# A transformer step on one core: the cross and feed-forward norms split into a gain ahead of the products and a root behind them, and their sums taken from GpSimd to VectorE

## The chip, the cores and the metric

The kernel runs on one core of a Trainium2 chip. Its engines are TensorE (matrix products, "PE" in the profile, its weight loads "PEld"), VectorE ("DVE"), ScalarE ("ACT"), GpSimd ("POOL") and SyncE ("SP", which issues the transfers). Each engine works through its own instructions in order and waits for the others by semaphores. The metric is the device time of one execution in microseconds. Three runs of the kernel before took 2624.62 to 2628.29 us, with a median of 2626.17.

## The reference, cut to what matters

One decoder layer for 2048 prompt tokens and 64 sample tokens, 1024 channels, all in float32:

```python
def _rmsnorm(x, g):
    return x * rsqrt(mean(x * x, axis=-1, keepdims=True) + 1e-5) * g

h = _rmsnorm(x, g_mix);  q, k, v, u = split(h @ w_in)          # windowed attention and pooling mixer
x = x + concatenate([attn_o, pool_o]) @ w_out
h = _rmsnorm(x, g_cross)
s = einsum('blhd,bmhd->bhlm', h @ w_cq, mem_k) * 256 ** -0.5   # 4 heads, 256 memory tokens
x = x + einsum('bhlm,bmhd->blhd', softmax(s), mem_v) @ w_co
h = _rmsnorm(x, g_ffn)
x = x + square(relu(h @ w_up)) @ w_down                        # hidden width 4096
y = _rmsnorm(x, g_final)
```

The root of a norm is one number per token. It is a factor of a whole row of `h`, so it can be applied to a product of `h` as well as to `h`: `(r * x * g) @ w = r * ((x * g) @ w)`. ReLU lets a positive factor through.

## The kernel before, in words

The tokens are cut into three superblocks of two blocks each: 384 + 384, 384 + 384, and 256 + (256 prompt and 64 sample) tokens. Activations lie with channels on the partitions and tokens along the columns. Every float32 product is made of three products of rounded parts: each operand is split into `hi` (a rounded copy) and `lo` (what is left), and hi x hi, hi x lo and lo x hi are added up in PSUM.

Weights come as 128x1024 pieces: a transfer into one of six `f` buffers, a cast on ScalarE (line 136, the `hi` part), and a subtraction on VectorE (line 137, the `lo` part), into two of twelve `w` buffers. `Stream` emits these ahead of the products that need them. When a dense stage has processed its last chunk, `S.behind` holds the residual add and the square of that chunk, and the casts emitted next are kept behind these two instructions (`issue_after`).

A superblock goes through these stages:

- norm 1 of both blocks, the "in" projection, windowed attention, pooling;
- `wo`, a dense stage of eight output chunks. A chunk of one block is 24 products (eight channel groups times three). `evac` of a chunk adds the product to `x` on VectorE (line 903) and calls `Norm.sq`;
- cross attention: per 128 tokens and pair of heads 24 products against the pieces "A" (the query weights and memory keys multiplied together beforehand), then a softmax: maximum (949) and its scale (950) on VectorE, exponentials on ScalarE (952), reciprocal (953), the scale of the probabilities on GpSimd (955), transposes on TensorE (931). The sample tokens have a path of their own;
- "B", a dense stage like `wo` (adds at line 1105);
- the feed-forward stage: eight groups of `up` (four chunks for both blocks) and `down`. The evacuation of an up chunk is ReLU on ScalarE (1143), its square on GpSimd (1144), a cast on ScalarE (1146) and a subtraction on VectorE (1147). The residual adds of `down` are line 1177. Norm 1 of the next superblock is worked in around `down(6)` and `down(7)`; the final norm (1194) follows `down(7)`.

A norm is built in three steps. `sq` squares a chunk on ScalarE (210) and adds it to an accumulator on GpSimd (211). `fin` sums the accumulator over the partitions with a product against a matrix of ones (220), then takes the root: logarithm and exponential on ScalarE (223, 224) and a correction step on VectorE (225 to 227). `apply` makes the operand of the next products: x times gain times root on VectorE (238), the `hi` cast on ScalarE (239), and the `lo` subtraction (241), which alternates between VectorE and GpSimd.

The order on each engine comes from a scheduler that places the instructions by the order of the program and by dependences; a few are pinned (`keep_in_program_order`, `issue_after`). `dense` goes through chunks and blocks as `order(nch, head, tail)` says: the first `head` chunks for block 0 and then for block 1, the middle ones in pairs, the last `tail` chunks again first for block 0 and then for block 1. What comes `after` a block (its `fin` and `apply`) is started one chunk after the block's last. There are four PSUM banks for dense products (`mm`), four for the rest (`aux`), eight `t` buffers of 400 columns for what VectorE, ScalarE and GpSimd pass on, and sixteen `act` buffers for operands.

Of the kernel before, what the change touches and what calls it, by code (L numbers as in the profile page):

```python
# [14 lines left out]
P = 128  # L15
# [36 lines left out]
def kernel(ctx: ExitStack, tc: tile.TileContext, io, nW=12, nF=6, nT=8):  # L52
# [30 lines left out]
    kcar = sb("kcar", 512, F32R)  # L83
    vt = sb("vt", 1024, F32R)
# [30 lines left out]
    class Stream:  # L115
        def __init__(self):
            self.items = deque()
            self.ready = deque()
            self.resW = 0
            self.resF = 0  # L120
            self.behind = []
# [4 lines left out]
        def emit(self):  # L126
# [6 lines left out]
            with ExitStack() as held:  # L133
                for i in self.behind:
                    held.enter_context(tc.issue_after(i))
                nc.scalar.copy(th[:], r[:, 0:1024])  # L136
                eng.tensor_tensor(tl[:], r[:, 0:1024], f32(th[:]), ALU.subtract)  # L137
# [50 lines left out]
    class Norm:  # L188
        def __init__(self, n, x, on_pe=False, add=None):
            self.n, self.x, self.on_pe, self.add = n, x, on_pe, add or nc.gpsimd  # L190
            self.acc = None
            self.pm = AUX.get() if on_pe else None

        def sq(self, k, eng=None):
            n = self.n
            i = None
# [11 lines left out]
            else:  # L208
                t = TS.get()
                i = nc.scalar.activation(t[:, 0:n], self.x(k), AF.Square)  # L210
                self.add.tensor_tensor(self.acc[:, 0:n], self.acc[:, 0:n], t[:, 0:n], ALU.add)  # L211
                TS.put(t)
            return i
# [17 lines left out]

        def apply(self, g, hi, lo, piece=8):
            n = self.n
            for k in range(8):
# [5 lines left out]
                eng = nc.vector if k % 2 == 0 else nc.gpsimd  # L240
                eng.tensor_tensor(lo(k), t[:, 0:n], f32(hi(k)), ALU.subtract)  # L241
                TS.put(t)
            TS.put(self.r)

# [28 lines left out]
    def dense(keys, blks, hi, lo, evac, head=2, tail=3, after=None, piece=8, seq=None):  # L273
# [3 lines left out]
        for c, b in seq or order(nch, head, tail):  # L277
# [13 lines left out]
            last = evac(c, b, ps)  # L291
            S.behind = last or []
# [75 lines left out]
    def prologue():  # L368
# [32 lines left out]
        for name, dst in (("ck", io["mk"]), ("cv", io["mv"])):  # L401
            a = Act(256)
            outs.append(a)
            for c in range(8):
                th, tl = S.next((name, c))
                ps = MM.get()
                if name == "ck" and c == 0:
                    with tc.issue_after(wu.ins):
                        mm3(ps[:, 0:256], range(8), lambda k: w8(th)[:, k, :], lambda k: w8(tl)[:, k, :], hm.hi, hm.lo)
                else:  # L410
# [80 lines left out]
    def superblock(s, blks, nxt):  # L491
# [409 lines left out]
        def add_evac(c, b, ps):  # L901
            bl = blks[b]
            i = nc.vector.tensor_tensor(bl.x(c), ps[:, 0:bl.n], bl.x(c), ALU.add)
            j = bl.norm.sq(c)
            return [i.ins, j.ins] if (c, b) == (7, 1) else None
# [13 lines left out]
        run(dense([("wo", s, c) for c in range(8)], blks, mix_hi(0), mix_hi(1), add_evac, head=3, after=after_out))  # L919
# [4 lines left out]
        def cross():  # L924
# [53 lines left out]
        def sample_cross():  # L978
# [11 lines left out]
            for i in range(2):  # L990
                nc.scalar.copy(qs[0:64, 512 * i:512 * i + 512], qq[i][0:64, :])
# [32 lines left out]
            nc.vector.tensor_scalar(t[:, 2:4], t[:, 0:2], -1.0 / 16, None, ALU.mult)  # L1024
            for g in range(2):
                nc.scalar.activation(pp[:, 256 * g:256 * g + 256], spv[:, g, :], AF.Exp, bias=t[:, 2 + g:3 + g], scale=1.0 / 16, accum_out=t[:, 4 + g:5 + g])
# [76 lines left out]
        def add_evac2(c, b, ps):  # L1103
            bl = blks[b]
            i = nc.vector.tensor_tensor(bl.x(c, 0, bl.np), ps[:, 0:bl.np], bl.x(c, 0, bl.np), ALU.add)  # L1105
            j = bl.norm.sq(c)
            return [i.ins, j.ins] if (c, b) == (7, 1) else None

        def after_co(b):
# [4 lines left out]
            bl.h3 = Act(bl.n)  # L1114
            yield from bl.norm.apply(V_GFFN, bl.h3.hi, bl.h3.lo, PIECE[2][b])

        for bl in blks:
            bl.norm = Norm(bl.n, bl.x)
            bl.nfull = bl.n
# [231 lines left out]
```

## Time and profile before

| | |
|---|---|
| median of three runs (lowest, highest) | 2626.17 us (2624.62, 2628.29) |
| profiled execution, its span | 2623.82 us, 2622.0 us |
| mean granted TensorE clock | 0.994 |
| TensorE busy | 2562.3 us, 98% |
| VectorE, ScalarE, GpSimd busy | 1300.5, 982.8, 657.9 us |
| squares of ReLU on GpSimd (1144) | 192 instructions, 216.4 us |
| sums of the norms on GpSimd (211) | 161 instructions, 182.2 us |
| bytes moved, mean rate | 244.76 MB, 93 GB/s |

In the rows of the profile "L211" is line 211, `t<-t,t` is the output and the inputs by the program's names, then partitions x elements and the type, then the count. A wait row names the waiting engine and line, then the engine and line that ended the wait, then the total, the number of times and the longest, in us. A window row begins with its start and end and its length, and then gives the busy time of PE, PEld, DVE, ACT and POOL with counts, the granted clock, the share of the DMA engines, and GB/s. A timeline row begins with start and duration.

### The profile page before, as it was taken

What the parts mean: (1) busy time and instruction counts of PE and PEld (TensorE: products, weight loads), DVE (VectorE), ACT (ScalarE), POOL (GpSimd) and SP (SyncE); (2) the same over time, 40 slices, a digit from 0 to 9 for tenths busy, and PEclk for the clock granted to TensorE, in tenths of its full rate; (3) what the DMA queues carried; (4) which work ended last, traced back from release to release, by engine and by line L of the source; (5) the groups of instructions that cost most, each with busy time, mean ns of one, the idle gap of its engine ahead of it and who ended that gap; (6) DMA issues with size and microseconds to landing.
All of it is one profiled execution on the core that took longest, in us unless ns stands there. A gap on an engine that the chain in (4) does not pass through costs nothing. (4 is left out here: it accounts for less than half of the span.)

```text
span 2622.0 us, 39268 instructions
## 1 busy us (share of the span) xinstructions
PE 2562.3 (98%) x15753; PEld 2457.1 (94%) x15753; DVE 1300.5 (50%) x2283; ACT 982.8 (37%) x1923; POOL 657.9 (25%) x723
## 2 busy tenths in 40 slices
PE   9899999999999999999999999999999999999998
PEld 8799989999999999897999999999999669999998
DVE  8567453533333367936363333334765645344334
ACT  6666342422222244824342222223464444322231
POOL 2215322411111152433241111113334214111111
PEclk9999999999999999999999999999999999999999
DMA  7833111211221123131111211112414572222210
GB/s 280 263 122 117 62 49 51 86 61 63 65 65 65 57 73 106 57 120 57 65 64 65 65 60 62 65 57 70 145 58 149 184 278 100 81 82 88 82 57 37
DMA packets 92539, 244.76 MB, mean 93 GB/s; under 512 B 16772, under 2 KB 31556, under 8 KB 91204
## 3 DMA queue, kind: packets, MB, share of 16 engines
q1 hardware_dynamic: 92356, 242.25, 27.9%
q8 instruction: 123, 2.02, 0.3%
q14 instruction: 60, 0.49, 0.1%
HBM read 219.53 MB, written 22.69 MB: 92 GB/s over the span
## 5 line engine op out<-in xcount | busy, mean ns | idle before, releaser
L286 PE MATMUL mm<-act,w 128*128 128x384 f32 (+2 forms) x2784 | 901.1, 324 | 2.8 <-ACT act L642 1.6
L287 PE MATMUL mm<-act,w 128*128 128x384 f32 (+2 forms) x2784 | 897.0, 322 | 3.4 <-POOL act L241 1.5
L288 PE MATMUL mm<-act,w 128*128 128x384 f32 (+2 forms) x2784 | 895.6, 322 | 1.4 <-DVE w L137 1.4
L136 ACT CAST w<-f 128x1024 fp32r<-128x1024 f32 x330 | 344.3, 1049 | 702.7 <-PE mm L112 457.6
L137 DVE TENSOR_TENSOR w<-f,w 128x1024 fp32r<-128x1024 f32 x330 | 418.4, 1276 | 305.7 <-ACT w L136 304.8
L111 PE MATMUL mm<-act,w 128*128 128x384 f32 (+2 forms) x1728 | 552.3, 320 | 2.8 <-DVE t L394 2.2
L113 PE MATMUL mm<-act,w 128*128 128x384 f32 (+2 forms) x1728 | 548.8, 318 | 1.9 <-DVE w L137 1.9
L112 PE MATMUL mm<-act,w 128*128 128x384 f32 (+2 forms) x1728 | 548.5, 317 | 0.0
L287 PEld LDWEIGHTS mm<-act,w 128*128 128x128 f32 x2784 | 525.7, 189 | 12.7 <-POOL act L241 3.7
L286 PEld LDWEIGHTS mm<-act,w 128*128 128x128 f32 x2784 | 525.8, 189 | 7.6 <-issue 2.3
L288 PEld LDWEIGHTS mm<-act,w 128*128 128x128 f32 x2784 | 525.6, 189 | 2.2 <-DVE w L137 2.0
L1144 POOL TENSOR_TENSOR t<-t 128x384 f32<-128x384 f32 (+2 forms) x192 | 216.4, 1127 | 1038.6 <-ACT t L1143 1038.6
L1177 DVE TENSOR_TENSOR x<-mm,x 128x384 f32<-128x384 f32 (+2 forms) x384 | 199.7, 523 | 327.5 <-PE mm L113 327.5
L111 PEld LDWEIGHTS mm<-act,w 128*128 128x128 f32 x1728 | 326.8, 189 | 4.7 <-ACT t L207 2.4
L113 PEld LDWEIGHTS mm<-act,w 128*128 128x128 f32 x1728 | 326.8, 189 | 2.4 <-DVE w L137 2.3
L112 PEld LDWEIGHTS mm<-act,w 128*128 128x128 f32 x1728 | 326.9, 189 | 1.1 <-issue 0.3
L211 POOL TENSOR_TENSOR t<-t,t 128x384 f32<-128x384 f32 (+2 forms) x161 | 182.2, 1132 | 337.0 <-ACT t L210 329.6
L1147 DVE TENSOR_TENSOR act<-t,act 128x384 fp32r<-128x384 f32 (+2 forms) x192 | 101.4, 528 | 295.5 <-ACT act L1146 295.4
L1146 ACT CAST act<-t 128x384 fp32r<-128x384 f32 (+2 forms) x192 | 93.5, 487 | 233.6 <-POOL t L1144 233.6
L210 ACT ACTIVATE t<-x 128x384 f32<-128x384 f32 (+2 forms) x140 | 68.0, 498 | 161.7 <-DVE x L1105 74.5
L111 PE MATMUL mm<-w,act 128*128 128x512 f32 x288 | 116.5, 407 | 9.7 <-ACT w L136 9.7
L1143 ACT ACTIVATE t<-mm 128x384 f32<-128x384 f32 (+2 forms) x192 | 88.3, 460 | 92.5 <-PE mm L288 88.6
(187 smaller groups left out, 2216.9 us busy)
## 6 DMA issues: line engine op xcount, KB each, us to landing
f<-in_wup SPq DMA_DIRECT2D x96, 512.0 KB, 3.5
f<-in_wdn SPq DMA_DIRECT2D x96, 512.0 KB, 3.5
f<-in_win SPq DMA_DIRECT2D x30, 512.0 KB, 3.8
f<-a_s SPq DMA_DIRECT2D x24, 512.0 KB, 3.5
f<-b_s SPq DMA_DIRECT2D x24, 512.0 KB, 4.7
x<-in_x SPq DMA_DIRECT2D x6, 1536.0 KB, 6.9
f<-in_wco SPq DMA_DIRECT2D x16, 512.0 KB, 5.4
f<-in_cmk SPq DMA_DIRECT2D x16, 512.0 KB, 4.3
```

The source lines that it names most:

```text
L111: nc.tensor.matmul(ps, Wh(k), Hh(k), start=first and i == 0, stop=False)
L112: nc.tensor.matmul(ps, Wh(k), Hl(k), start=False, stop=False)
L113: nc.tensor.matmul(ps, Wl(k), Hh(k), start=False, stop=final and i == last)
L136: nc.scalar.copy(th[:], r[:, 0:1024])
L137: eng.tensor_tensor(tl[:], r[:, 0:1024], f32(th[:]), ALU.subtract)
L211: self.add.tensor_tensor(self.acc[:, 0:n], self.acc[:, 0:n], t[:, 0:n], ALU.add)
L286: nc.tensor.matmul(ps[:, 0:n], w8(th)[:, k, :], hi(b, k), start=k == 0, stop=False)
L287: nc.tensor.matmul(ps[:, 0:n], w8(th)[:, k, :], lo(b, k), start=False, stop=False)
L288: nc.tensor.matmul(ps[:, 0:n], w8(tl)[:, k, :], hi(b, k), start=False, stop=k == 7)
L1144: nc.gpsimd.tensor_tensor(q[:, 0:n], r[:, 0:n], r[:, 0:n], ALU.mult)
L1147: nc.vector.tensor_tensor(lo, q[:, 0:n], f32(hi), ALU.subtract)
L1177: nc.vector.tensor_tensor(bl.x(m), ps[:, 0:n], bl.x(m), ALU.add)
```

## The change: what it does

For the cross and the feed-forward norm `apply` is gone. The evacuation of each `wo` and `B` chunk now also makes the operand of the next stage from gain times `x`, without the root: `hi` on ScalarE and `lo` on VectorE (`gain`). The root comes in behind the products. For the cross stage `fin_cols` makes it as a column per 128 tokens (one-column products with the accumulator as weights) and it becomes the scale of the exponentials and of the maximum; the sample queries are scaled by it when they are copied. For the feed-forward stage the root stays a tile (`r3`, in one of the eight `t` buffers for each block through the whole stage), and VectorE takes maximum with zero and times root in one instruction; the square moves from GpSimd to ScalarE. All sums of all norms go from GpSimd to VectorE, and in norm 1 all `lo` subtractions are on VectorE. The weight casts are no longer held behind the last square. `wo` has tail 2 (before 3), `B` tail 2 (before 4), `up(0)` head 2 (before 4).

```diff
-            with ExitStack() as held:
-                for i in self.behind:
-                    held.enter_context(tc.issue_after(i))
-                nc.scalar.copy(th[:], r[:, 0:1024])
-                eng.tensor_tensor(tl[:], r[:, 0:1024], f32(th[:]), ALU.subtract)
+            nc.scalar.copy(th[:], r[:, 0:1024])
+            eng.tensor_tensor(tl[:], r[:, 0:1024], f32(th[:]), ALU.subtract)
...
-            self.n, self.x, self.on_pe, self.add = n, x, on_pe, add or nc.gpsimd
+            self.n, self.x, self.on_pe, self.add = n, x, on_pe, add or nc.vector
...
+        def fin_cols(self, c):
+            pm = AUX.get()
+            w = (self.n + P - 1) // P
+            for i in range(w):
+                m = min(P, self.n - P * i)
+                tc.keep_in_program_order(nc.tensor.matmul(pm[0:m, i:i + 1], self.acc[:, P * i:P * i + m], ones[:, 0:1], start=True, stop=True))
+            TS.put(self.acc)
...
+            v, y, t = c[:, 8:8 + w], c[:, 12:12 + w], c[:, 16:16 + w]
+            nc.scalar.activation(t, v, AF.Ln, bias=eps[:])
+            nc.scalar.activation(y, t, AF.Exp, scale=-0.5)
...
+            nc.vector.tensor_scalar(c[:, 0:w], y, 1.0 / 16, None, ALU.mult)
+            nc.vector.tensor_scalar(c[:, 4:4 + w], y, -1.0 / 16, None, ALU.mult)
...
-                eng = nc.vector if k % 2 == 0 else nc.gpsimd
-                eng.tensor_tensor(lo(k), t[:, 0:n], f32(hi(k)), ALU.subtract)
+                nc.vector.tensor_tensor(lo(k), t[:, 0:n], f32(hi(k)), ALU.subtract)
...
+    def gain(bl, act, k, g):
+        gk = vec[:, g + k:g + k + 1]
+        nc.scalar.activation(act.hi(k), bl.x(k), AF.Copy, scale=gk)
+        nc.vector.scalar_tensor_tensor(act.lo(k), bl.x(k), gk, f32(act.hi(k)), ALU.mult, ALU.subtract)
...
-            i = nc.vector.tensor_tensor(bl.x(c), ps[:, 0:bl.n], bl.x(c), ALU.add)
-            j = bl.norm.sq(c)
-            return [i.ins, j.ins] if (c, b) == (7, 1) else None
+            nc.vector.tensor_tensor(bl.x(c), ps[:, 0:bl.n], bl.x(c), ALU.add)
+            gain(bl, bl.h2, c, V_GCROSS)
+            bl.norm.sq(c)
...
-            bl.norm.fin()
             ACTS.put(*bl.q, *bl.d)
-            bl.h2 = Act(bl.n)
-            yield from bl.norm.apply(V_GCROSS, bl.h2.hi, bl.h2.lo, 8 if last and b else PIECE[1][b])
+            bl.rc = RC[b]
+            bl.norm.fin_cols(bl.rc)
...
-                        nc.vector.tensor_scalar(t[:, 2:4], t[:, 0:2], -1.0 / 16, None, ALU.mult)
+                        i = c0 // P
+                        nc.vector.tensor_scalar(t[:, 2:4], t[:, 0:2], bl.rc[:, 4 + i:5 + i], None, ALU.mult)
                         for h in range(2):
-                            nc.scalar.activation(Pt[:, 256 * h:256 * h + 256], psv[:, h, :], AF.Exp, bias=t[:, 2 + h:3 + h], scale=1.0 / 16, accum_out=t[:, 4 + h:5 + h])
+                            nc.scalar.activation(Pt[:, 256 * h:256 * h + 256], psv[:, h, :], AF.Exp, bias=t[:, 2 + h:3 + h], scale=bl.rc[:, i:i + 1], accum_out=t[:, 4 + h:5 + h])
...
-            bl.h3 = Act(bl.n)
-            yield from bl.norm.apply(V_GFFN, bl.h3.hi, bl.h3.lo, PIECE[2][b])
+            bl.r3 = bl.norm.r
...
-                nc.scalar.activation(r[:, 0:n], ps[:, 0:n], AF.Relu)
-                nc.gpsimd.tensor_tensor(q[:, 0:n], r[:, 0:n], r[:, 0:n], ALU.mult)
+                nc.vector.scalar_tensor_tensor(r[:, 0:n], ps[:, 0:n], 0.0, bl.r3[:, 0:n], ALU.max, ALU.mult)
+                nc.scalar.activation(q[:, 0:n], r[:, 0:n], AF.Square)
```

The order of the instructions moves with it. In these listings a number behind a name is that of the buffer, and the lines of the changed kernel are its own. ScalarE at the end of `wo` in superblock 0, before: the squares of chunks (L210), the `hi` casts of the norm (L239) and then the three weight casts for "A" (L136).

```order
L210 ACTIVATE t_100<-x_106 128x384
L239 CAST act_76<-t_102 128x384
L239 CAST act_76<-t_98 128x384
L239 CAST act_76<-t_104 128x384
L239 CAST act_76<-t_101 128x384
L210 ACTIVATE t_97<-x_106 128x384
L136 CAST w_79<-f_92 128x1024
L136 CAST w_87<-f_93 128x1024
L136 CAST w_88<-f_94 128x1024
```

The same place in the changed kernel, where L206 is the square, L133 the weight cast, L266 the gain, and L243 and L244 are the root as a column:

```order
L206 ACTIVATE t_101<-x_105 128x384
L266 ACTIVATE act_76<-x_105,vec 128x384
L206 ACTIVATE t_97<-x_105 128x384
L133 CAST w_87<-f_93 128x1024
L266 ACTIVATE act_64<-x_106,vec 128x384
L206 ACTIVATE t_99<-x_106 128x384
L243 ACTIVATE rc_132<-rc_132,eps 128x3
L244 ACTIVATE rc_132<-rc_132 128x3
L133 CAST w_88<-f_94 128x1024
L266 ACTIVATE act_64<-x_106,vec 128x384
L206 ACTIVATE t_102<-x_106 128x384
```

The cast into `w_87` now stands ahead of the last two gains and squares, the cast into `w_88` ahead of the last one, and the cast into `w_79` further ahead than is shown.

VectorE at the end of superblock 0, before: the final norm of block 0 (L1194, eight instructions), residual adds of block 1 (L1177) and weight splits (L137); the sums are on GpSimd.

```order
L227 SCALAR_TENSOR_TENSOR t_103<-t_98,t_103 128x384
L1194 SCALAR_TENSOR_TENSOR x_105<-x_105,vec,t_103 128x384 x8
L1177 TENSOR_TENSOR x_106<-mm_107,x_106 128x384
L1177 TENSOR_TENSOR x_106<-mm_108,x_106 128x384
L1177 TENSOR_TENSOR x_106<-mm_109,x_106 128x384
L137 TENSOR_TENSOR w_82<-f_96,w_83 128x1024
L137 TENSOR_TENSOR w_84<-f_91,w_85 128x1024
L97 TENSOR_TENSOR w_80<-mm_110,w_79 64x384
```

The same place in the changed kernel, where L1199 is the residual add, L1216 the final norm, L134 the split and L207 a sum:

```order
L222 SCALAR_TENSOR_TENSOR t_103<-t_100,t_103 128x384
L1199 TENSOR_TENSOR x_106<-mm_107,x_106 128x384
L1216 SCALAR_TENSOR_TENSOR x_105<-x_105,vec,t_103 128x384 x8
L207 TENSOR_TENSOR t_101<-t_101,t_102 128x384
L1199 TENSOR_TENSOR x_106<-mm_108,x_106 128x384
L1199 TENSOR_TENSOR x_106<-mm_109,x_106 128x384
L134 TENSOR_TENSOR w_82<-f_96,w_83 128x1024
L207 TENSOR_TENSOR t_101<-t_101,t_104 128x384
L134 TENSOR_TENSOR w_84<-f_91,w_85 128x1024
L207 TENSOR_TENSOR t_101<-t_101,t_99 128x384
```

Three sums of block 1 now stand between its last residual adds and the weight splits, and one add has gone ahead of the final norm of block 0.

More of the change, by code (lines that the diff above doesn't have):

```diff
@@ L83 @@
     kcar = sb("kcar", 512, F32R)
+    RC = [sb(f"rc{i}", 20) for i in range(2)]
     vt = sb("vt", 1024, F32R)
@@ L290, in dense @@
                     yield
-            last = evac(c, b, ps)
-            S.behind = last or []
+            evac(c, b, ps)
             MM.put(ps)
@@ L406, in prologue @@
                 ps = MM.get()
[L407 to L410, printed above, removed]
+                with ExitStack() as held:
+                    if (name, c) == ("ck", 0):
+                        held.enter_context(tc.issue_after(wu.ins))
                     mm3(ps[:, 0:256], range(8), lambda k: w8(th)[:, k, :], lambda k: w8(tl)[:, k, :], hm.hi, hm.lo)
@@ L911, in after_out @@
             bl = blks[b]
[L912 removed]
             ACTS.put(*bl.q, *bl.d)
[L914 to L915 removed]
+            bl.rc = RC[b]
+            bl.norm.fin_cols(bl.rc)
         for bl in blks:
             bl.norm = Norm(bl.n, bl.x)
[L919 removed]
+            bl.h2 = Act(bl.n)
+        run(dense([("wo", s, c) for c in range(8)], blks, mix_hi(0), mix_hi(1), add_evac, head=3, tail=2, after=after_out))
         for bl in blks:
@@ L1104, in add_evac2 @@
             bl = blks[b]
-            i = nc.vector.tensor_tensor(bl.x(c, 0, bl.np), ps[:, 0:bl.np], bl.x(c, 0, bl.np), ALU.add)
-            j = bl.norm.sq(c)
-            return [i.ins, j.ins] if (c, b) == (7, 1) else None
+            nc.vector.tensor_tensor(bl.x(c, 0, bl.np), ps[:, 0:bl.np], bl.x(c, 0, bl.np), ALU.add)
+            gain(bl, bl.h3, c, V_GFFN)
+            bl.norm.sq(c)
         def after_co(b):
```

28 lines of the change are left out of this document (18 added, 10 removed).

## The prediction

> **What bounds the kernel now.** I first read the page's busy line and the list of what the engines wait for.
>
> ```profile
> PE 2562.3 (98%) x15753; PEld 2457.1 (94%) x15753; DVE 1300.5 (50%) x2283; ACT 982.8 (37%) x1923; POOL 657.9 (25%) x723
> ```
>
> TensorE computes for 2562.3 of the 2622.0 us, and the change leaves it the same large products. So only the 59.7 us in which TensorE is idle, and any small products added, can move the time. Next I read TensorE's waits (total, times, longest), whole span:
>
> ```profile
> PE mm L111 <- ACT w L136: 9.9, 7, 3.0
> PE aux L220 <- POOL t L211: 7.9, 4, 2.7
> PE aux L931 <- POOL cp L955: 2.5, 4, 0.8
> ```
>
> The second row is the sum of a norm, still being added up on GpSimd when TensorE reaches the product that reads it. The first row is weight casts that come too late, and the third is softmax tiles. The same view by window says where. First the start of the cross stage (from 300 us in superblock 0, from 1190 in 1; both have this row):
>
> ```profile
> PE mm L111 <- ACT w L136: 2.4, 1, 2.4
> ```
>
> The start of the cross stage in superblock 2 (2036 to 2062 us):
>
> ```profile
> PE mm L112 <- DVE w L137: 2.3, 1, 2.3
> PE aux L112 <- DVE act L974: 1.3, 1, 1.3
> PE mm L111 <- ACT w L136: 0.7, 1, 0.7
> PE aux L113 <- POOL act L241: 0.6, 1, 0.6
> ```
>
> The start of the feed-forward stage in superblock 2 (2188 to 2212); the same place in superblocks 0 and 1 has the third row alone, with the same 0.5:
>
> ```profile
> PE aux L220 <- POOL t L211: 1.4, 1, 1.4
> PE mm L287 <- DVE act L241: 0.8, 2, 0.4
> PE mm L287 <- POOL act L241: 0.5, 1, 0.5
> PE mm L286 <- ACT act L239: 0.2, 1, 0.2
> ```
>
> The two block ends, where the next superblock's first norms and the final norm run under the last down products: at 985 to 1012 us
>
> ```profile
> PE aux L220 <- POOL t L211: 1.3, 1, 1.3
> PE mm L286 <- DVE x L1177: 0.5, 1, 0.5
> ```
>
> and at 1860 to 1885 the first of these two rows again with 2.5 (the second is the same, 0.5):
>
> ```profile
> PE aux L220 <- POOL t L211: 2.5, 1, 2.5
> ```
>
> Last the prologue, at 66 to 82 us the sum, and at 98 to 114 the weights:
>
> ```profile
> PE aux L220 <- POOL t L211: 2.7, 1, 2.7
> ```
>
> ```profile
> PE mm L111 <- ACT w L136: 3.5, 2, 3.0
> PE mm L112 <- DVE w L137: 0.8, 1, 0.8
> ```
>
> All of these except the last two rows are waits for work that the change removes, shortens or moves.
>
> **The change part by part.**
>
> *The cross norm no longer stands between wo and the cross products.* ScalarE's timeline shows why the weight cast is late:
>
> ```profile
> 319.13 0.52 ACT L210 ACTIVATE t<-x 128x384 f32<-128x384 f32 x1 [0.49 <-DVE x L903]
> 319.56 2.93 ACT L136 CAST w<-f 128x1024 fp32r<-128x1024 f32 x3
> ```
>
> The three casts are held behind the last square. Afterwards one is done before, the next stands ahead of the last two gains and squares, and none is held, so the 2.4 us go twice. The L931 waits (2.5 us in all, these two superblocks) come from softmax steps queued on VectorE among the eight L238 and eight L241 of the second block. Those are gone; I take all 2.5. Sum 7.3. In superblock 2 the same hold and the same norm cost 0.7 + 2.3 + 1.3 + 0.6 = 4.9. There I leave 0.5, because a late gain on ScalarE now stands ahead of the last sample cast: 4.4.
>
> *The feed-forward norm.* All rows of L220, L241 and L239 before the up products go: 1.4 + 0.8 + 0.5 + 0.2 + 2 x 0.5 = 3.9. The up products start on gain times x; the root is first needed by VectorE one chunk later.
>
> *The sums on VectorE.* Seven sums of 256 columns ran there before (minimum, median, maximum ns):
>
> ```profile
> L211 DVE TENSOR_TENSOR t<-t,t x7: 418/422/425, 6.7 to 16.6; 128x256 f32<-128x256 f32 x7
> ```
>
> and a two-input instruction of 384 columns, the residual add, takes (sum, mean ns):
>
> ```profile
> L1177 DVE TENSOR_TENSOR x<-mm,x 128x384 f32<-128x384 f32 x256 | 141.4, 556 | 232.0 <-PE mm L113 232.0
> ```
>
> Both read two tensors and write one, so I take 0.556 us for a sum of 384 columns. The block end is the place where VectorE is short. Busy times there (PE, PEld, DVE, ACT, POOL), then its groups from 930 to 1010 us:
>
> ```profile
> 930.00:966.00 36.00, 36.00 (x207) 35.73 (x207) 24.93 (x38) 13.71 (x25) 17.25 (x16) 1.00 0.31 89
> 966.00:1000.00 34.00, 34.00 (x194) 33.29 (x193) 27.03 (x39) 15.18 (x27) 19.13 (x18) 1.00 0.29 102
> 1000.00:1010.00 10.00, 8.27 (x45) 7.48 (x44) 8.31 (x12) 4.41 (x9) 5.32 (x6) 1.00 0.53 182
> ```
>
> ```profile
> L238 DVE SCALAR_TENSOR_TENSOR t<-f,vec,t 128x384 f32<-128x384 f32 x16 | 15.4, 992 | 1.0 <-POOL t L211 0.9
> L137 DVE TENSOR_TENSOR w<-f,w 128x1024 fp32r<-128x1024 f32 x7 | 12.6, 1814 | 3.9 <-ACT w L136 3.9
> ```
>
> and what GpSimd has there, 23 sums and 8 subtractions:
>
> ```profile
> L211 POOL TENSOR_TENSOR t<-t,t 128x384 f32<-128x384 f32 x23 | 28.3, 1229 | 14.6 <-ACT t L210 13.8
> L241 POOL TENSOR_TENSOR act<-t,act 128x384 fp32r<-128x384 f32 x8 | 9.5, 1191 | 15.8 <-ACT act L239 15.8
> ```
>
> VectorE is busy 24.9 + 27.0 + 8.3 = 60.3 of 80 us. Moved to it are 31 instructions at 0.556, 17.2 us. But its own rows are stretched here: outside this stretch, from 500 to 900 us, L137 takes
>
> ```profile
> L137 DVE TENSOR_TENSOR w<-f,w x48: 1224/1226/1227, 504.2 to 895.2; 128x1024 fp32r<-128x1024 f32 x48
> ```
>
> 1.226 against 1.814. With GpSimd quiet I expect 7 x 0.59 = 4.1 us back there and, if L238 falls to the same 0.556, 16 x 0.44 = 7.0 more, so 60.3 + 17.2 - 11.1 = 66 of 80: still room. The mechanism shows in the feed-forward stage, one VectorE split and two GpSimd squares:
>
> ```profile
> 504.19 1.23 DVE L137 TENSOR_TENSOR w<-f,w 128x1024 fp32r<-128x1024 f32 x1 [2.48 <-ACT w L136]
> ```
>
> ```profile
> 504.62 1.48 POOL L1144 TENSOR_TENSOR t<-t 128x384 f32<-128x384 f32 x1 [4.05 <-ACT t L1143]
> 508.07 0.83 POOL L1144 TENSOR_TENSOR t<-t 128x384 f32<-128x384 f32 x1 [1.97 <-ACT t L1143]
> ```
>
> The square takes 0.83 alone and 1.48 when it starts inside a split. [...]
>
> Laying the new VectorE order on these durations, the residual add that frees a bank at 1000 us ends near 1000.0 instead of 1000.5, and the second block's last sum near 1004.0. TensorE's rows there:
>
> ```profile
> 1004.76 0.34 PE L288 MATMUL mm<-act,w 128*128 128x384 f32 x1
> 1006.37 0.91 PE L220 MATMUL aux<-t,ones 128*128 128x384 f32 x2 [1.27 <-POOL t L211]
> 1006.83 0.63 PE L286 MATMUL mm<-act,w 128*128 128x384 f32 x1
> ```
>
> TensorE gets there at about 1004.9, or 1004.4 without the earlier wait: a margin of half a microsecond. Of the block ends' 1.3 + 0.5 + 2.5 + 0.5 = 4.8 us I take 4.0. In the prologue I take half of 2.7, 1.4: the weights are late anyway a little later (3.5 + 0.8 us above), and that does not change.
>
> *Restarts.* L220 starts 1.61 us after the row before it, at a usual spacing of 0.174 (207 products in the first 36.00 us above), while the wait counts 1.27: 0.17 more per wait, and the rows behind run slow. For some 20 waits removed, 3.
>
> *The root as a column.* In the cross norm one 384-column sum product (two passes; 1006.37 to 1006.83, 0.46 us) becomes three one-column ones, six passes, six times in the kernel. The narrowest fp32 product in the trace:
>
> ```profile
> 1922.50 1.97 PE L812 MATMUL aux<-t,f 128*128 128x32 f32 x16
> 1925.04 3.43 PE L812 MATMUL aux<-t,f 128*128 128x32 f32 x16
> ```
>
> Sixteen in 1.97 or 3.43 us: about 0.11 to 0.21 each, so 0.7 to 1.25 per norm instead of 0.46. I take 0.4 more each, 2.4 in all (bounds 1.2 and 4.8). [...]
>
> *At nothing.* 192 ReLUs times root on VectorE (0.556, like L1177) take the place of ScalarE's; a chunk of 24 products at 0.174 is 4.2 us, and VectorE has there 0.556 + 0.556 + half a split 0.61 = 1.7 of them. Four banks cover a ReLU up to three chunks late; without that cover each would cost its 0.556, 107 us in all. Per wo chunk VectorE has add, gain, sum and half a split, 2.3 of 4.2. The gain on ScalarE waits for its chunk's add; behind it stand the chunk's square and a weight cast that TensorE needs only chunks later. The squares go to ScalarE where the ReLUs were. No transfer is moved. Shorter heads and tails keep fewer weight buffers, no more DMA. For stalls not seen I add 1.0.
>
> Sum: 7.3 + 4.4 + 3.9 + 4.0 + 1.4 + 3 = 24.0 gained, 2.4 + 1.0 lost: 20.6 us. The profiled execution took 2623.8, 2.4 under the median of the runs, 2626.2; I take the 20.6 from the median: **2605.6, say 2606**.
>
> **The rivals.**
>
> *Only the clean half.* VectorE's queue is fuller wherever norms and weight splits meet, and what the sums gain in the prologue, at the block ends and in superblock 2 is lost again by adds and splits queued behind them. Left are 7.3 + 3.9 + half of 4.4 + half the restarts = 14.9, less 3.4: 11.5, so about 2615. For it speaks the half microsecond of margin; against it, the 66 of 80.
>
> *More.* The column products hide (0) and every listed wait goes, the prologue's in full: 7.3 + 4.9 + 3.9 + 4.8 + 2.7 + 3 = 26.6, so about 2600, and 2597 if the softmax tiles and attention also run ahead with a quieter GpSimd. Against it: the prologue's weights.
>
> *VectorE becomes the bound at the block ends: slower.* If the 23 sums cost there what L238 costs now, 0.99, and nothing gets shorter, VectorE has 60.3 + 22.8 + 8 x 0.556 = 87.5 us of work in 80; adds wait, banks stay taken, TensorE loses 7.5 us at each of two block ends, and as an estimate as much again in the prologue, where two norms are summed too: 22.5 lost. Of the 20.6 the 4.0 and the 1.4 of these places are not gained: 15.2. That is 7.3 slower, 2633. It decides once a moved instruction costs over (80 - 60.3) / 31 = 0.64 us. Against it: the 0.42 and 0.556 rows.
>
> *Nothing that can be measured.* The waits pass on to the next late thing, the weight stream: 2624. Against it: outside the prologue only the held casts make weights late.
>
> **How the numbers follow.** Forecast 0.50 (2599 to 2611), clean half 0.24, more 0.14, slower 0.06, nothing 0.06. 0.2% of 2626 is 5.2 us, about what a measurement of this kernel can tell from no change: faster means under 2621. Forecast, more and five sixths of the clean half are faster: 0.84; same: the rest of the clean half and nothing, 0.10; slower 0.06. The range is 2596 to 2621: it takes in the clean half with some of its spread and most of "more", and leaves out the two last cases.
>
> **What would show it.** Right: the L220 rows released by L211 and the L241 rows are gone from TensorE's waits; L111's wait for L136 loses its 2.4 us twice; GpSimd falls from 658 to below 200 us, VectorE rises to about 1440; the new sums take 0.556 and L137 at the block end returns to 1.23; TensorE's idle falls from 60 to some 40 us. Wrong: waits of TensorE for VectorE's x or sums near 1000 and 1875 us, one-column products above 0.2 us each, or gains on ScalarE ahead of weight casts that TensorE waits for.

## The result, and the profile after

The changed kernel takes 2590.38 us, the median of four runs from 2587.93 to 2594.30; the kernel before took 2627.14 beside it. The ratio is 0.9862 with an interval of 0.9847 to 0.9876. It is 36.8 us faster, where 20.6 had been forecast, and lies below the range. The profiled execution has a span of 2592.5 us, 29.5 less than before; a second one of the same kernel has 2589.4, against 2623.8 for a second one of the kernel before.

The page of the changed kernel:

```profile
PE 2554.5 (99%) x15775; PEld 2459.0 (95%) x15775; DVE 1385.8 (53%) x2632; ACT 997.9 (38%) x1923; POOL 175.8 (7%) x298
```

GpSimd fell to 176 us, VectorE rose by 85 instead of the 140 forecast, and TensorE's idle time went from 59.7 to 38.0 us. TensorE's waits, the longest groups:

```profile
PE aux L709 <- DVE st L710: 3.0, 7, 0.9
PE mm L112 <- ACT w L373: 2.7, 1, 2.7
PE aux L740 <- POOL x L731: 2.5, 3, 1.5
PE mm L112 <- DVE t L417: 2.4, 1, 2.4
PE mm L112 <- ACT w L133: 2.4, 2, 1.8
```

All sums, all subtractions of a norm and the late casts at the cross stage are gone from the list; what is left is mostly the prologue and the attention. To see where the time went I cut both executions at the start of each cross stage and at the end of each block. The windows from the start of the cross stage to the end of the superblock (length, then PE, PEld, DVE, ACT, POOL busy), before:

```profile
313.70:1032.10 718.40, 712.29 (x3999) 694.14 (x3998) 319.31 (x459) 225.55 (x393) 170.74 (x167) 1.00 0.22 69
1188.40:1903.90 715.50, 708.13 (x4023) 690.80 (x4023) 314.91 (x472) 222.64 (x396) 165.00 (x167) 1.00 0.23 72
2035.70:2622.00 586.30, 565.69 (x4081) 524.63 (x4079) 263.95 (x443) 189.33 (x343) 116.16 (x124) 0.99 0.32 111
```

and after:

```profile
317.20:1025.80 708.60, 708.28 (x4004) 694.01 (x4003) 340.54 (x550) 222.64 (x379) 18.45 (x36) 1.00 0.21 69
1182.90:1887.60 704.70, 704.38 (x4028) 690.44 (x4027) 337.52 (x564) 219.61 (x382) 17.21 (x36) 1.00 0.23 71
2019.60:2592.50 572.90, 560.28 (x4086) 522.59 (x4084) 275.00 (x511) 188.08 (x328) 12.26 (x22) 0.99 0.33 112
```

These three became 9.8 + 10.8 + 13.4 = 34.0 us shorter (33.8 in the second pair of profiles; two profiles of one kernel agree to 0.2 us in their sum). The prologue, the projections and `wo` together became 4.5 longer in this pair and 0.6 shorter in the second, so they change little and vary by several us between executions of one kernel. In the three, TensorE's idle time fell from 34.1 to 13.3 us, 20.8 less: the waits that the prediction had listed. The other 13.2 us are busy time of TensorE, for the same large products. That is what the forecast had not seen. Its place shows in windows of 2 us around the wait at the start of the cross stage before; the third number from the end is the granted clock:

```profile
318.00:320.00 2.00, 0.24 (x1) 0.00 (x0) 1.03 (x3) 1.38 (x3) 1.20 (x2) 1.00 0.00 0
320.00:322.00 2.00, 1.36 (x4) 1.00 (x5) 1.38 (x2) 2.00 (x3) 0.79 (x1) 0.75 0.00 0
322.00:324.00 2.00, 2.00 (x6) 1.63 (x6) 2.00 (x2) 0.48 (x1) 0.00 (x0) 0.50 0.47 131
324.00:326.00 2.00, 2.00 (x9) 1.47 (x8) 1.00 (x3) 0.62 (x2) 0.00 (x0) 0.89 0.82 277
```

and in two products inside and two behind this stretch (TensorE's timeline):

```profile
321.78 0.63 PE L113 MATMUL mm<-w,act 128*128 128x512 f32 x1
322.21 0.63 PE L112 MATMUL mm<-w,act 128*128 128x512 f32 x1
...
327.54 0.39 PE L113 MATMUL mm<-w,act 128*128 128x512 f32 x1
327.77 0.39 PE L111 MATMUL mm<-w,act 128*128 128x512 f32 x1
```

Behind the wait of 2.4 us the clock is granted at half for 3.4 us, and the products follow one another every 0.43 us instead of 0.23. The same happened in the kernel before near 1195 and 2045 us, behind waits of 2.4 and 2.3 us, and near 2209 us, behind three waits of 0.2 to 0.5 us within 2 us; in the changed kernel at none of these places. The rows of the page gave only "9" for all forty slices of the clock, and the prediction had read no finer.

### The profile page after: what moved, and what is told of

The parts are those of the page before. It is cut to its first block, busy times and chain, and to the rows that moved or that the text cites. A ratio compares the mean times of both kernels' runs of the same rounds, so it can differ in the third digit from the quotient of the medians.

```text
span 2592.5 us, 38981 instructions
## 1 busy us (share of the span) xinstructions
PE 2554.5 (99%) x15775; PEld 2459.0 (95%) x15775; DVE 1385.8 (53%) x2632; ACT 997.9 (38%) x1923; POOL 175.8 (7%) x298
## 5 line engine op out<-in xcount | busy, mean ns | idle before, releaser
L133 ACT CAST w<-f 128x1024 fp32r<-128x1024 f32 x330 | 346.0, 1050 | 828.9 <-PE mm L113 499.0
L134 DVE TENSOR_TENSOR w<-f,w 128x1024 fp32r<-128x1024 f32 x330 | 402.7, 1225 | 129.4 <-ACT w L133 127.4
L1199 DVE TENSOR_TENSOR x<-mm,x 128x384 f32<-128x384 f32 (+2 forms) x384 | 200.0, 522 | 326.4 <-PE mm L114 326.4
L1165 DVE SCALAR_TENSOR_TENSOR t<-mm,t 128x384 f32<-128x384 f32 (+1 forms) x192 | 100.6, 524 | 285.7 <-PE mm L312 285.7
L1166 ACT ACTIVATE t<-t 128x384 f32<-128x384 f32 (+1 forms) x192 | 95.0, 495 | 251.4 <-DVE t L1165 251.4
L1169 DVE TENSOR_TENSOR act<-t,act 128x384 fp32r<-128x384 f32 (+1 forms) x192 | 100.1, 521 | 103.9 <-ACT act L1168 103.9
L112 PE MATMUL mm<-w,act 128*128 128x512 f32 x288 | 115.0, 403 | 1.9 <-ACT w L133 1.8
L113 PE MATMUL mm<-w,act 128*128 128x512 f32 x288 | 113.6, 395 | 1.6 <-DVE w L134 1.6
L114 PE MATMUL mm<-w,act 128*128 128x512 f32 x288 | 113.3, 394 | 0.0
L266 ACT ACTIVATE act<-x,vec 128x384 fp32r<-128x384 f32 (+2 forms) x96 | 56.3, 587 | 111.1 <-DVE x L925 57.5
```

Of the source, the lines that this page charges most:

```text
L112: nc.tensor.matmul(ps, Wh(k), Hh(k), start=first and i == 0, stop=False)
L113: nc.tensor.matmul(ps, Wh(k), Hl(k), start=False, stop=False)
L114: nc.tensor.matmul(ps, Wl(k), Hh(k), start=False, stop=final and i == last)
L1165: nc.vector.scalar_tensor_tensor(r[:, 0:n], ps[:, 0:n], 0.0, bl.r3[:, 0:n], ALU.max, ALU.mult)
L1166: nc.scalar.activation(q[:, 0:n], r[:, 0:n], AF.Square)
L1169: nc.vector.tensor_tensor(lo, q[:, 0:n], f32(hi), ALU.subtract)
```

## The experiments

### The two kernels again

No edit; second profiles of both.

> The changed kernel unaltered, for a second profile. Theory A (clock): besides the waits themselves, TensorE runs at half its clock for some 3.5 us after some of them, about 1.7 us lost each time; where it falls differs between executions, so the stretches of half clock of the first profile (near 25, 97, 127, 253 and 1909 us, 10 us of clock time) are partly at other places, and the time moves with their number. Theory B (waits alone): the time lost is the waits plus a restart of 0.2 to 0.3 us each; the profile shows the same waits and the same time within 1 us. Both: a median near 2590.

> The kernel before unaltered, for a second profile. Theory A: the stretches of half clock behind the 2.4 us waits at the start of the cross stage (near 321 and 1195 us) and at 74, 2044 and 2208 us come again at most of these places, 1.7 us each, but not at all. Theory B: no loss behind a wait beyond 0.3 us.

The changed kernel: 2591.66 us (2589.26 to 2593.63), ratio 0.9866 with 0.9852 to 0.9879. Ahead of the program's end half clock stood near 26, 126, 1908 and 1955 us; in the first profile near 26, 97, 127, 254 and 1911. So it does move between executions of one kernel, above all in the prologue. In the kernel before it came again near 322, 2046 and 2210, but not near 1195, though the wait is the same. The second profile there:

```profile
1194.00:1196.00 2.00, 0.56 (x2) 0.19 (x1) 1.36 (x3) 1.06 (x3) 0.96 (x2) 1.00 0.00 0
1196.00:1198.00 2.00, 1.03 (x4) 0.67 (x4) 1.05 (x1) 2.00 (x3) 1.05 (x2) 1.00 0.00 0
1198.00:1200.00 2.00, 1.91 (x9) 1.40 (x8) 2.00 (x3) 0.81 (x1) 0.00 (x0) 1.00 0.37 106
```

Theory A holds so far: a wait of 2.4 us can bring half clock and need not. Superblock 1 from its cross stage on, with the same waits in both, is 714.6 us long here and 715.5 in the first profile.

### One part alone: the hold, the sums

The hold taken away from the kernel before:

```diff
-            S.behind = last or []
+            S.behind = []
```

> The kernel before with one edit: weight casts are no longer held behind the last square. Theory A: the two 2.4 us waits of L111 for L136 go, and with them the half clock behind both (1.7 us each): about 8 to 9 us faster. Theory B: 4.8 to 5.5 us faster. If the casts come no earlier because ScalarE is busy with the norm's own casts ahead of them: no change.

It took 2633.99 us (2632.25 to 2637.95), ratio 1.0029 with 1.0018 to 1.0041: slower, where both theories said faster. TensorE's waits:

```profile
PE aux L220 <- POOL t L211: 20.5, 9, 3.7
PE mm L111 <- ACT w L136: 3.9, 4, 1.9
```

The casts do come earlier (9.9 to 3.9 us), but their splits then stand on VectorE ahead of the last residual add, and the last square and sum are late instead (7.9 to 20.5). VectorE in this kernel at the end of B in superblock 0:

```profile
460.11 4.00 DVE L137 TENSOR_TENSOR w<-f,w 128x1024 fp32r<-128x1024 f32 x2
464.02 0.55 DVE L1105 TENSOR_TENSOR x<-mm,x 128x384 f32<-128x384 f32 x1
```

The add waits out two splits of 2.0 us each, stretched as they were at the block end. So the hold had been right for the kernel before.

The sums and subtractions moved, in the kernel before:

```diff
-            self.n, self.x, self.on_pe, self.add = n, x, on_pe, add or nc.gpsimd
+            self.n, self.x, self.on_pe, self.add = n, x, on_pe, add or nc.vector
...
-                eng = nc.vector if k % 2 == 0 else nc.gpsimd
+                eng = nc.vector
```

> The kernel before with one edit: all sums of norms, and norm 1's subtractions, on VectorE instead of GpSimd (the subtractions of the other norms too). Both theories: the waits of L220 for L211 (7.9 us) go. Theory A: the half clock near 74 us goes too, about 8 to 11 us faster; theory B: 8 to 9 us. My slower rival (VectorE becomes the bound at the block ends): not faster, with waits of TensorE for x near 1000 and 1875 us.

It took 2608.91 us (2607.31 to 2610.31), ratio 0.993 with 0.9916 to 0.9943: 17.4 us faster than the kernel before beside it, over one and a half times what either theory had. The three stretches of its profile are 19.0 us shorter than in the kernel before. Its waits, the first and the one for casts:

```profile
PE aux L931 <- POOL cp L955: 4.2, 10, 0.7
...
PE mm L111 <- ACT w L136: 2.1, 3, 0.9
```

With the hold still in place, no wait for L136 is left at the start of the cross stage, and no half clock behind it. The cast had been late because the square ahead of it was late, and the square because VectorE's part of the norm was stretched beside GpSimd's. VectorE's products of x, gain and root from 300 to 330 us, in the kernel before and here:

```profile
L238 DVE SCALAR_TENSOR_TENSOR t<-x,vec,t 128x384 f32<-128x384 f32 x11 | 9.4, 896 | 0.2
L238 DVE SCALAR_TENSOR_TENSOR t<-x,vec,t 128x384 f32<-128x384 f32 x10 | 5.8, 617 | 0.0
```

The edit moves sums and subtractions together, so their shares are not told apart.

### One part undone in the changed kernel

Sums back on GpSimd (the first line above, turned round):

> The changed kernel with one part undone: all sums of norms on GpSimd again. If the sums are what made the block ends and the stage starts late (the kernel before with only the sums moved gained 17 us), then the waits of TensorE's sum product for GpSimd come back: 8 to 20 us slower than the changed kernel, 2600 to 2611. If the split of the norm into gain and root made them harmless except at the block ends and in the prologue: 7 to 9 us slower, 2598 to 2600. My prediction's own terms for the sums (4.0 + 1.4 us): 2596.

It took 2600.25 us (2596.37 to 2603.88), ratio 0.9898 with 0.9879 to 0.9916: some 9 us slower than the changed kernel. The wait returns, at the two block ends and once in superblock 2:

```profile
PE aux L215 <- POOL t L207: 4.3, 3, 2.5
```

So the split into gain and root makes late sums nearly harmless at the stage starts, though not at the block ends, where norm 1 is as before. The 4.3 us of waits are half of the 9; one stretch of half clock stands behind the 2.5 us wait, near 1868, and another near 2100, behind a wait of 2.0 us for a transfer.

The hold put back:

```diff
-            evac(c, b, ps)
+            last = evac(c, b, ps)
+            S.behind = last or []
...
```

> The changed kernel with one part undone: weight casts held behind the last residual add and square of wo and B again. My prediction's term for the hold (2.4 us twice, 0.7 and a restart): 5 to 7 us slower, 2597. The other theory: the hold only cost because the last square was late, VectorE being slowed beside GpSimd's sums, and costs nothing now: 2589 to 2593, and no wait of L112 for L133 at the start of the cross stage.

It took 2590.29 us (2587.99 to 2593.99), ratio 0.9865 with 0.9851 to 0.9880: no difference. The hold neither costs nor helps once the last square is early.

The feed-forward part undone (norm between B and up, ReLU on ScalarE and square on GpSimd, head and tail 4):

```diff
-            gain(bl, bl.h3, c, V_GFFN)
...
-            bl.r3 = bl.norm.r
+            bl.h3 = Act(bl.n)
+            yield from bl.norm.apply(V_GFFN, bl.h3.hi, bl.h3.lo, PIECE[2][b])
...
-                nc.vector.scalar_tensor_tensor(r[:, 0:n], ps[:, 0:n], 0.0, bl.r3[:, 0:n], ALU.max, ALU.mult)
-                nc.scalar.activation(q[:, 0:n], r[:, 0:n], AF.Square)
+                nc.scalar.activation(r[:, 0:n], ps[:, 0:n], AF.Relu)
+                nc.gpsimd.tensor_tensor(q[:, 0:n], r[:, 0:n], r[:, 0:n], ALU.mult)
...
```

> The changed kernel with the feed-forward norm's part undone: the whole norm stands again between B and up, ReLU on ScalarE and its square on GpSimd, head and tail as before; the cross norm and the sums stay changed. By my term for this part (3.9 us and restarts): 5 to 6 us slower, 2596. If with the sums on VectorE the norm is early anyway: 0 to 2 us slower. If the freed GpSimd matters in the whole stage: 10 and more.

It took 2595.85 us (2593.11 to 2597.07), ratio 0.9877 with 0.9860 to 0.9893: by the medians 4 to 5 us slower than the changed kernel, near the prediction's term, though the intervals of the two overlap. In the profiles the three stretches are 4.5 to 4.8 us longer than in the changed kernel, all but 0.3 of it in superblock 2. There one wait of 1.3 us for the `hi` cast returns and one of 0.3 us for the sum; in superblocks 0 and 1 none does. So the size came out, but not the waits that the term was made of; where the rest of it lies is open.

### Made waits

Does a wait of TensorE itself bring half clock, and from what length? The first two attempts did not make waits. The first let VectorE pass over a chunk's weights before the chunk (once, or four times):

```diff
+            if keys[0][0] == "up" and (c, b) == (1, 0) and keys[0][2] % 2 == 1:
+                for _ in range(4):
+                    nc.vector.scalar_tensor_tensor(th[:, 0:384], prev[:, 0:384], 0.0, f32(th[:, 0:384]), ALU.mult, ALU.add)
```

> The changed kernel with 12 made waits of TensorE (before one up chunk in every second group, its weights pass once more through VectorE, after the chunk before it is finished): some 1.3 us each. Theory A (half clock behind a wait that is long enough): these are too short, so the time grows by the waits and a restart each, 12 x 1.6 = 19 us, no more than one or two stretches of half clock. Theory B (waits alone): the same 19.

> The same with four passes through VectorE in place of one: waits of some 3.0 us, 12 times. Theory A: most of them bring a stretch of half clock at 1.7 us lost: 12 x 3.3 + 8 to 12 x 1.7 = 53 to 60 us slower than the changed kernel, with the stretches right behind the waits. Theory B: 12 x 3.3 = 40 us slower.

They took 2591.39 and 2597.49 us, with no wait of the products concerned over 0.2 us: the scheduler had moved other products in between. The second attempt put 14 or 24 passes inside a chunk:

```diff
+                if made and k == 4:
+                    pm = AUX.get()
+                    tc.keep_in_program_order(nc.tensor.matmul(pm[:, 0:P], ones[:], ident[:], start=True, stop=True))
+                    for _ in range(14):
+                        nc.vector.scalar_tensor_tensor(th[:, 512:640], pm[:, 0:P], 0.0, f32(th[:, 512:640]), ALU.mult, ALU.add)
...
```

> The changed kernel with 21 made waits inside an up chunk (group 1 to 7 of each superblock): 14 passes of VectorE over the weights of one channel group, started by a small product put in order ahead of the chunk; the four channel groups before it cover some 2 us, so TensorE should wait 0.7 to 1.6 us each. Theory A (half clock behind a wait that is long enough): waits this short bring a stretch of half clock at no more than a third of the sites: 21 x 1.4 = 30 us by waits and restarts, plus up to 7 x 1.7. Theory B (waits and restarts alone): 30 us slower than the changed kernel, whatever the length of the wait.

> The same with 24 passes: waits of 2 to 4 us each. Theory A: nearly every site is followed by a stretch of half clock, 1.7 us lost each: the time grows by the listed waits plus 21 x 0.3 plus 25 to 36 us. Theory B: by the listed waits plus 21 x 0.3 only.

They took 2598.30 and 2606.21 us. In the first no wait at these sites is listed, in the second only 8.2 us for residual adds (seven times, 1.2 at most), and in neither is there half clock in the feed-forward stages; again other products filled the place. These four say nothing on the clock beyond this: 4 to 132 us more of busy time on VectorE did not bring it in these stages.

The third attempt pinned the products of `up` and `down` in program order, so that nothing could fill the gap. The long one has nine passes, the short one two:

```diff
+                if made and k == 4:
+                    pm = AUX.get()
+                    pin(nc.tensor.matmul(pm[:, 0:P], ones[:], ident[:], start=True, stop=True))
+                    for _ in range(9):
+                        nc.vector.scalar_tensor_tensor(th[:, 512:640], pm[:, 0:P], 0.0, f32(th[:, 512:640]), ALU.mult, ALU.add)
+                    AUX.put(pm)
...
```

> The changed kernel with 21 made waits that nothing can fill: TensorE's products of the up and down stages are pinned in program order, and in the third chunk of groups 1 to 7 the fifth channel group's weights pass twice through VectorE behind a small product in the middle of the chunk: waits of about 1 us each. Theory A (half clock behind a wait that is long enough): no more than a third of the sites are followed by a stretch of half clock. Theory B (waits and restarts alone): none. Both: the waits listed, plus 0.3 us of small products and a restart of 0.2 to 0.3 at each site: about 30 to 35 us slower than the changed kernel.

> The same with nine passes: waits of about 2.5 to 3 us each. Theory A: at least 15 of the 21 sites are followed by a stretch of half clock of some 3.4 us, 1.7 us lost each: against the kernel with the short waits the time grows by the difference of the listed waits and by 25 to 36 us more. Theory B: by the difference of the listed waits alone (about 21 x 1.8 = 38 us), to 2 us.

The short one took 2635.67 us (2632.11 to 2638.18), the long one 2720.68 (2715.18 to 2727.26); their profiled spans are 2636.4 and 2713.4. The short one is some 45 us slower than the changed kernel, not 30 to 35; among its waits is one that was not made, 10.0 us in all for the squares of a norm, and the long one has it too (10.1). The made waits in the short one, then in the long one:

```profile
PE mm L320 <- DVE w L318: 23.5, 21, 1.5
```

```profile
PE mm L320 <- DVE w L318: 71.3, 21, 3.8
```

Behind none of the 21 short waits (0.92 to 1.52 us) is there half clock. Behind 20 of the 21 long ones (3.2 to 3.8 us) there is; the second of them:

```profile
578.00:580.00 2.00, 0.43 (x1) 0.43 (x2) 1.38 (x5) 0.00 (x0) 0.00 (x0) 0.84 0.56 227
580.00:582.00 2.00, 2.00 (x8) 2.00 (x8) 0.00 (x0) 0.00 (x0) 0.00 (x0) 0.50 0.04 8
```

and the one exception, the first:

```profile
508.00:510.00 2.00, 0.68 (x4) 0.68 (x5) 1.16 (x4) 0.00 (x0) 0.00 (x0) 1.00 0.42 172
510.00:512.00 2.00, 2.00 (x13) 2.00 (x12) 0.30 (x1) 0.00 (x0) 0.00 (x0) 1.00 0.04 8
```

In 2 us there are 13 products at full clock and 8 at half. The spans differ by 77.0 us, the listed waits by 71.3 - 23.5 = 47.8; the other 29.2 are 1.46 on average for each of the 20, in the 25 to 36 that theory A had (the medians differ by 85.0, which would leave 37). Two neighbouring sites say the same: the site with the exception is 70.2 us ahead of the next, later ones are 71.7 apart, with equal waits: 1.5 us for one stretch of half clock. Theory B falls.

### A version that beats both

```diff
-                nc.gpsimd.tensor_tensor(dt[:, 0:16], src[:, 0:16], rc, ALU.mult)
-                nc.gpsimd.tensor_tensor(dt[:, 0:16], dt[:, 0:16], ucur[:, 0:16], ALU.subtract)
+                nc.vector.tensor_tensor(dt[:, 0:16], src[:, 0:16], rc, ALU.mult)
+                nc.vector.tensor_tensor(dt[:, 0:16], dt[:, 0:16], ucur[:, 0:16], ALU.subtract)
...
-                nc.gpsimd.tensor_tensor(t[:, 0:L], src[:, step:step + L], src[:, 0:L], ALU.add)
+                (nc.vector if g == CIN[-1] - 6 else nc.gpsimd).tensor_tensor(t[:, 0:L], src[:, step:step + L], src[:, 0:L], ALU.add)
...
-                nc.gpsimd.tensor_scalar(Lv[:, i, :], Lv[:, i, :], t[:, 32 + i:33 + i], 1.0, ALU.mult, ALU.mult)
+                nc.vector.tensor_scalar(Lv[:, i, :], Lv[:, i, :], t[:, 32 + i:33 + i], 1.0, ALU.mult, ALU.mult)
...
-                    later.append([DEFF[bl.b], lambda bl=bl: final(bl)])
+                    later.append([1 if last else DEFF[bl.b], lambda bl=bl: final(bl)])
```

> The changed kernel with five small moves against waits that its profile still lists: the two 16-column corrections of the pooling mixer and its last channel group's window sums from GpSimd to VectorE (TensorE waits 1.6 us for ScalarE's L664 behind them), the sample probabilities' scale from GpSimd to VectorE (1.4 us behind L810), and the last superblock's first final norm started one step earlier, so that it is out of the way of the last residual adds (about 1 us). If each wait goes: 3 to 4 us faster than the changed kernel, 2587, more by 1.7 where a stretch of half clock goes with it. If VectorE is too full there: no change.

It took 2585.98 us (2582.51 to 2589.15), ratio 0.9842 with 0.9827 to 0.9857: 4 to 6 us faster than the two medians of the changed kernel, with intervals that overlap. Its three stretches are 3.0 us shorter, all in superblock 2. The listed wait for L664 fell from 1.6 to 0.4 us, that for L810 is gone, and its profile has half clock at two places ahead of the program's end, 124 and 1903 us, against four or five.

## Why the prediction was wrong in size

**The listed waits: right.** In the three stretches 19.6 us were taken (7.3 + 4.4 + 3.9 + 4.0); idle time fell by 20.8. Every discount there was unneeded.

**Restarts: the step that failed.** The prediction had 3 us for what is lost behind the waits, 0.17 for each. The three stretches lost 13.2 us of busy time, four times as much. It was worked out product by product: each start in TensorE's timeline against the usual spacing for its width, with the listed waits taken off. In the four stretches of half clock before the products start 1.4 to 1.7 us late each, about 6 us together, and after there are none; the second pair has three against none, about 5 us. Elsewhere in the three stretches the starts that are late by more than 0.08 us add up to 7.7 us more before than after, in the second pair 7.5. Examples stand at waits: 0.27 on top of the listed 2.4 us at 320.64 and 0.26 behind it, and seven of 0.1 to 0.3 around the one listed 0.5 at the start of the feed-forward stage of superblock 0. Which of these are restarts and which are waits too short for the list is not told apart. So the prediction saw that "the rows behind run slow" and put no price on it.

The row that it showed for this, at 1006.83, is no example. In the changed kernel the product behind the same sum product takes 0.63 us at 1000.54 as well, and no wait stands there.

The step is worth 10 us. The two pairs of profiles beat the 20.6 by 9 and 14, the medians by 16; what differs between these lies mostly ahead of the stretches, in the part that varies, and is not settled.

The rows to price it from were in the trace: at these four places (from 321.01, 1194.82, 2044.74 and 2208.58 us) the granted clock is 0.50 for 3.41 us each. As an estimate from these, four times half of 3.41 us, 6.8, would have gone into the sum.

**Which edit takes away the 2.4 us twice: wrong.** It was put down to the hold. The hold alone made the kernel slower, put back it costs nothing, and the sums and subtractions alone took the wait away. That VectorE's rows get shorter once GpSimd is quiet, which the prediction used at the block end alone, holds at the end of `wo` too (L238, 0.90 and 0.62 us above).

**The sums on VectorE: right.** At the block end in the changed kernel (groups, then the sum of three windows over the same 80 us of work):

```profile
L207 DVE TENSOR_TENSOR t<-t,t 128x384 f32<-128x384 f32 x27 | 14.9, 553 | 2.5 <-ACT t L206 1.9
L134 DVE TENSOR_TENSOR w<-f,w 128x1024 fp32r<-128x1024 f32 x7 | 8.6, 1221 | 1.3 <-ACT w L133 1.3
```

```profile
sum 80.00, PE 80.00 PEld 78.94 DVE 65.72 ACT 35.11 POOL 6.09; mean PE 26.67 PEld 26.31 DVE 21.91 ACT 11.70 POOL 2.03
```

A sum takes 0.553 us (0.556 taken), a split 1.221 (1.23), and VectorE 65.7 of 80 (66); only the products of x, gain and root take 0.61 (0.556). TensorE has no idle time there at all. The margin was wider than the half microsecond forecast: the last sum ends at 998.2 us and the product that reads it starts at 1000.2; at the second block end they are 0.9 us apart. The slower rival falls with these rows: its point of decision was 0.64 us for a moved instruction.

**The prologue: wrong, by 1.4 us.** The sum's wait of 2.7 us went, but the attention behind it began as late as before. The first part of the program, up to the attention, ends at 156.4 and 158.0 us in the two profiles before and at 158.4 and 157.2 after: the waits for its weights from 66 to 135 us grew from 5.8 to 7.1 us in the first pair, and two stretches of half clock stand there (97 and 127 us) against one before (75). That the weights set the end is argued from this; no run tests it.

**The one-column products: a size too large.** The prediction took 2.4 us. In the changed kernel:

```profile
312.41 0.72 PE L233 MATMUL aux<-ones,t 128*128 128x1 f32 x6
313.00 0.42 PE L310 MATMUL mm<-act,w 128*128 128x384 f32 x1
```

Six passes in 0.59 us, 0.10 each, against 0.46 for the sum product: 0.8 us at most in all six norms. The lower bound was nearest. The prediction read its row of sixteen in 1.97 us as 0.11 each; it is 0.12.

**The ReLU on VectorE: right; the feed-forward norm: right in size.** No wait of TensorE for the ReLU is listed. The part undone cost 4 to 5 us, but in superblock 2 alone and with only 1.6 us of the waits that the 3.9 were added up from, so that the size is partly luck.

So of the rivals the one that said more was nearest, but it put its 26.6 us on waits and the same 3 us behind them, and stopped at 2597. What was missed was not a listed wait but what is lost around it.

## What to carry to other kernels

Price a wait of TensorE by the time that the work behind it loses too: look at the granted clock in windows of a microsecond or two behind the waits and behind runs of short ones (here half clock came behind a wait of 1.6 us, and behind three of 0.2 to 0.5 within 2 us), since the page's forty slices of 66 us hid dips of 3.4 us, and take the same wait from two profiles. A wait names the instruction that came last, not the cause: the late cast stood behind a late square, which stood behind an engine slowed by its neighbour, and taking away the hold alone moved the stall to a worse place. Moving GpSimd's instructions to a busy VectorE beside it can cost less than their count says: here, with the sums and subtractions moved, VectorE's own splits at the block end went from 1.81 to 1.22 us.

## What the runs showed of the hardware that was not expected

Half clock came behind 0 of 21 waits of 0.9 to 1.5 us, 20 of 21 of 3.2 to 3.8 us, and at 2.4 us in three of the four cases at the start of the cross stage in superblocks 0 and 1. In the long kernel a stretch lasts 3.4 us behind 15 of these 20 waits; at five of the seven sites in superblock 2, with waits of 3.8 us, it lasts 6.8.

The length of a wait does not decide by itself. In the first profile of the kernel before TensorE is busy for 30, 46 and 31% of the 3.41 us that end where the stretches at 321.01, 1194.82 and 2044.74 us begin, and for 66% ahead of the one at 2208.58. The wait near 1195 us, in the first profile of the kernel before and then in the second:

```profile
1191.41:1194.82 3.41, 1.56 (x6) 0.67 (x4) 2.37 (x4) 1.68 (x4) 2.31 (x3) 1.00 0.00 0
```

```profile
1192.48:1195.89 3.41, 2.08 (x8) 1.06 (x7) 2.88 (x5) 1.67 (x5) 2.09 (x2) 1.00 0.00 0
1195.89:1199.31 3.42, 2.26 (x9) 1.56 (x10) 2.36 (x3) 2.92 (x4) 1.16 (x2) 1.00 0.02 7
```

In the first, with half clock behind it, TensorE is busy for 46% of the window; in the second the same wait is shared by two windows with 61 and 66%, and no half clock follows. A wait of 1.6 us near 250 us is followed by half clock in the first profile of the changed kernel (from 253.34 us) and not in those of the short and the long kernel, and one of 3.0 us that ends near 111 us in the first profile of the kernel before is not.

Half clock also came where TensorE did not wait: in the first profile of the kernel before from 1925.27 us for 6.83 us, with TensorE busy through all of the 3.41 us ahead, products of 32 columns among them; in the first profile of the changed kernel the same from 1908.80. What decides where it falls was not shown.

At a block end 17 us of work moved to VectorE raised its busy time there by 5.
